# The first stage of a two-layer trunk in a written order on four engines

## The chip, the cores and the metric

The kernel runs on one core of one Trainium2 chip. The metric is the device time of one execution in microseconds (us); lower is better. Before the change the median of three runs is 1106.1 us (1105.2 to 1107.23). TensorE (PE) multiplies matrices, ScalarE (ACT) applies functions and copies, VectorE (DVE) does elementwise work, GpSimd (POOL) sets memory, SyncE's queue (SP) issues the loads.

## What is computed

Two layers over 512 tokens of width 1024. Each layer is a token mixer and a SwiGLU feed-forward, each between two norms and with a shift, a scale and a gate from a condition `c`. Only the opening of layer 0 is touched:

```
shift, scale, gate = split(silu(c) @ w + b)      # w: 1024 x 3072
h = rms_norm(x, g) * (1 + scale) + shift         # x: 512 x 1024
qkv = h @ w_qkv                                  # then stick-breaking attention
```

## The kernel before, in words

Every product is made in three passes: an operand is split into a high half (ScalarE copies it to fp32r) and a low half (VectorE subtracts the high one from the original), and `mm3` multiplies high by high, high by low and low by high.

The first stage makes, from x and c, the transposed and modulated h (eight blocks of 128 columns, each 128x512, as high and low half), and multiplies it at once: half of v (four banks, 512 columns each, for the four token tiles) and q and k of the first pair of heads (one bank each). So each of the eight blocks k has twelve passes for v (`v_step`, L706) and six for q and k (`qk0_step`, L795), all 128x128 by 128x512.

- `norm0` (L678) squares a token tile of x on ScalarE, takes the root (`rms`, L467), and scales the tile on VectorE. `turn0` (L687) turns all eight of its 128x128 blocks on TensorE into two banks and copies them to the tiles `xhT` on ScalarE (VectorE for half of the first two token tiles).
- The scale and shift of a block are sums over the 1024 rows of an ada weight, weighted by silu(c). For blocks 0 and 1, `row0` (L764) does the sum on TensorE: sixteen instructions (eight calls) with a one-column operand, a copy of the row to SBUF, and two small products that turn it; `scales` (L777) adds and multiplies. For blocks 2 to 7, in pairs, `ada0_sum` (L740) sums on VectorE, eight steps of 512 columns into one accumulator, and `cols0` (L748) and `sums0` (L754) turn it with small products on TensorE; a VectorE product gives `ab`.
- `h0` (L784) writes h (high half) and x once more with scale and shift, both on ScalarE, and the low half on VectorE.
- Loads are issued by `load` (L125) from SyncE's queue. Weights pass through `wload` and `wemit` (L144, L154): a raw tile of 512 KB (two buffers), high half, low half.
- `bg0` is a background job (`Bg`, L397) that sums the gate of layer 0 in eight VectorE steps of 1024 columns, a few steps at a time; its loads come three steps ahead.

The framework orders instructions of one engine by program order and readiness. A helper keeps an order by hand where its `chain` flag is set: `dve`, `act` and `pe_op` (L64 to L101) tie each instruction to the one before on that engine. Before the change no chain is on in the first stage.

Around the stage, `for b in range(1, 4)` at L820 runs over the pairs of blocks; the loop over k = 6, 7 behind it finishes the products. Then v, q and k are copied out, and the second v half starts.

Of the kernel before, what the change touches and what calls it, by code (L numbers as in the profile page):

```python
# [13 lines left out]
P = 128  # L14
# [19 lines left out]
def trunk(ctx: ExitStack, tc: tile.TileContext, A: dict, out: bass.AP):  # L34
# [85 lines left out]
    def mm3(o, lh, ll, rh, rl, start, stop):  # L120
        mm(o, lh, rh, start, False)
        mm(o, lh, rl, False, False)
        mm(o, ll, rh, False, stop)

    def load(dst, src):  # L125
        nc.sync.dma_start(out=dst, in_=src)

    def split(hi, lo, src, hi_dve=False):
        if hi_dve:
# [24 lines left out]
    def wemit():  # L154
        n = len(got)
        src, a, b, key = stream[n]
        if len(raws) == n:
            wload()
        if src is None:
            if not first_blocks or n > first_blocks[-1] + KF:  # L160
                first_blocks.append(n)
            for _ in blocks(*next_raws(n)):
                pass
            return
        raw = raws[n]
        if key[0] == "wdn" and key[2] in SEVEN[key[1]]:
            got.append(down_blocks(raw))
            return
        h, l = wtile(a, b, SHORT if key[0] in ("wgu", "win_u") else 16)
        if key[0] == "wqk" and key[1]:  # L170

            act.activation(h[:], raw[:], AF.Copy)
            nc.vector.tensor_tensor(l[:], raw[:], h[:].bitcast(F32), ALU.subtract)
            if len(raws) == n + 1 and stream[n + 1][3][0] == "wqk":
                wload()
        else:
            high = act.activation(h[:], raw[:], AF.Copy)
            last_low[0] = nc.vector.tensor_tensor(l[:], raw[:], h[:].bitcast(F32), ALU.subtract)  # L178
# [178 lines left out]

    cT = consts.tile([P, KD], F32, name="cT")
    load(cT[:], A["c"])
    x0, a0 = [], []  # L360
    for tt in range(NT):
        xt = slot(F32, "x0", 1, 1024)
        load(xt[:, 0, :], A["x"][tt * P : (tt + 1) * P, :])
        x0.append(xt[:, 0, :])
        if tt == 0:
            identt = consts.tile([P, P], F32, name="identt")
            load(identt[:], A["consts"][:, 0, :])
            cols = consts.tile([P, 4, KD], F32, name="cols")
            load(cols[:], A["cols"])
        elif tt == 3:  # L370
            a0.extend(ada0_raw(0, q) for q in range(2))
    wload()
# [294 lines left out]


    add = consts.tile([P, KD, 2], F32, name="add")
    dve.tensor_copy(add[:, :, 1], cols[:, 1, :])  # L670
    dve.tensor_scalar(add[:, :, 0], cols[:, 0, :], 1.0, None, ALU.add)
    mul = consts.tile([P, KD, 2], F32, name="mul")
    dve.memset(mul[:, :, 1], 1.0)
    dve.tensor_copy(mul[:, :, 0], cols[:, 2, :])

    xhT = [slot(F32, "xhT") for _ in range(4)]

    def norm0(tt):  # L678
        xt = x0[tt]
        junk = npool.tile([P, D], F32, tag="n", name=nm("junk"))  # L680
        sx = small.tile([P, 1], F32, tag="sx", name=nm("sx"))
        act.activation(junk[:], xt, AF.Square, accum_out=sx[:])
        sd, r1 = rms(sx[:])
        dve.reciprocal(r1[:], sd[:])
        dve.tensor_scalar(xt, xt, r1[:, 0:1], None, ALU.mult)

    def turn0(tt):  # L687
        xt = x0[tt]
        for q in range(2):
            ps = bank("tp0")  # L690
            for k in range(4):
                kk = q * 4 + k
                transpose(ps[:, k * P : (k + 1) * P], xt[:, kk * P : (kk + 1) * P])
            for k2 in range(2):
                dst = xhT[q * 2 + k2][:, :, tt * P : (tt + 1) * P]
                src = ps[:, k2 * 256 : (k2 + 1) * 256].rearrange("p (a b) -> p a b", a=2)
                if q and tt < 2:
                    dve.tensor_copy(dst, src)
                else:
                    act.activation(dst, src, AF.Copy)  # L700

    hT = new_hT()

# [33 lines left out]

    onec = oneb[:, 0:1]

    def ada0_sum(raws, n, nk, tag="acch"):  # L740
        acc = adas.tile([P, 512], F32, tag=tag, name=nm("acc"))
        nc.gpsimd.memset(acc[:, :n], 0.0)
        for q, raw in enumerate(raws):
            for k in range(nk):
                ada_stt(acc[:, :n], raw[:, k, :], q * nk + k)
        return acc

    def cols0(k):  # L748

        ps = bank("ab0", "p")  # L750
        mm(ps[:, 0:4], ident, add[:, k : k + 2, :].rearrange("p n a -> p (n a)"), True, False)
        return ps

    def sums0(ps, acc, k):  # L754

        for i in range(4):
            mm(ps[:, i : i + 1], acc[:, i * P : (i + 1) * P], onec, False, i == 3)
        ab = small.tile([P, 2, 2], F32, tag="ab", name=nm("ab"))
        dve.tensor_tensor(
            ab[:], ps[:, :4].rearrange("p (n a) -> p n a", a=2), mul[:, k : k + 2, :], ALU.mult  # L760
        )
        return ab

    def row0(raws):  # L764

        ps = bank("ab0", "p")
        for q, raw in enumerate(raws):
            for k in range(4):
                mm(ps[0:1, :256], sc[:, q * 4 + k : q * 4 + k + 1], raw[:, k, :], q + k == 0, q * 4 + k == 7)
        row = stp.tile([P, 256], F32, tag="row", bufs=2, name=nm("row"))  # L770
        dve.tensor_copy(row[0:1, :], ps[0:1, :256])
        ps = bank("ab0", "p")
        for i in range(2):
            mm(ps[:, i : i + 1], row[0:1, i * P : (i + 1) * P], oneb[0:1, 0:1], True, True)
        return ps

    def scales(ps, k):  # L777

        ab = small.tile([P, 2, 2], F32, tag="ab", name=nm("ab"))
        dve.tensor_tensor(ab[:, 0, :], ps[:, :2], add[:, k, :], ALU.add)  # L780
        dve.tensor_tensor(ab[:, 0, :], ab[:, 0, :], mul[:, k, :], ALU.mult)
        return ab

    def h0(ab, i, k):  # L784

        xk = xhT[k // 2][:, k % 2, :]
        h, l = hTk(hT, k, 0, T)
        for out in (h, xk):
            act.activation(out, xk, AF.Identity, scale=ab[:, i, 0:1], bias=ab[:, i, 1:2])
        dve.tensor_tensor(l, xk, h.bitcast(F32), ALU.subtract)  # L790

    wv0, wqk0 = [], []

    def qk0_step(k):
        for w, pb in zip(wqk0, (pq0, pk0)):  # L795
            h, l = hTk(hT, k, 0, T)
            mm3(pb[:], w[0][:, k, :], w[1][:, k, :], h, l, k == 0, k == KD - 1)

    norm0(0)
    norm0(1)  # L800
    turn0(0)
    norm0(2)
    ab0 = row0(a0)
    turn0(1)
    norm0(3)
    turn0(2)
    turn0(3)
    wv0.append(wget(("wv", 0, 0), 0))
    a2 = [ada0_raw(2, q) for q in range(4)]
    h0(scales(ab0, 0), 0, 0)  # L810
    ab1 = row0(a1)
    wqk0.append(wget(("wqk", 0, 0), 0))
    vb = [bank("v0") for _ in range(NT)]
    pq0, pk0 = bank("pq"), bank("pk")
    v_step(vb, 0, 0, wv0[0])
    h0(scales(ab1, 1), 0, 1)
    wqk0.append(wget(("wqk", 0, 1), 0))
    wload()
    acc = ada0_sum(a2, 512, 2)
    for b in range(1, 4):  # L820

        ps = cols0(2 * b)
        if b > 1:
            v_step(vb, 0, 2 * b - 2, wv0[b - 1])
        qk0_step(2 * b - 2)
        an = [ada0_raw(b + 2, q) for q in range(4)] if b < 3 else []
        if b == 1:
            v_step(vb, 0, 1, wv0[0])
        ab = sums0(ps, acc, 2 * b)
        h0(ab, 0, 2 * b)  # L830
        wv0.append(wget(("wv", 0, b), 0))
        h0(ab, 1, 2 * b + 1)
        if b < 3:
            wload()
            acc = ada0_sum(an, 512, 2, ("acch", "accl")[b % 2])
        if b > 1:
            v_step(vb, 0, 2 * b - 1, wv0[b - 1])
        if b == 2:
            bg0.step(3)
        qk0_step(2 * b - 1)  # L840
        if b == 3:
            bg0.step(1)
    for k in (6, 7):
        v_step(vb, 0, k, wv0[3])
        bg0.step(1)
        qk0_step(k)
        bg0.step(1)
# [9 lines left out]
    with tc.tile_pool(name="att", bufs=1) as att, tc.tile_pool(name="att2", bufs=2) as att2:  # L857
# [196 lines left out]
        for k in range(KD):  # L1054
            if k % 2 == 0:
                wv = wget(("wv", 1, k // 2))
            v_step(vb, 1, k, wv)
            if k in (3, 5):
                cur[0](B31 if k == 3 else B2)
            if k in (1, 2, 6):  # L1060
                bg0.step(1)
# [615 lines left out]
```

## Time and profile before

| | |
|---|---|
| span of the profiled execution | 1104.6 us |
| runs | 1106.1 us median, 1105.2 to 1107.23 |
| busy: TensorE, VectorE, ScalarE, GpSimd | 98%, 86%, 54%, 3% |
| first transpose on TensorE | 7.84 us |
| first v product | 23.72 us |
| first product of the second v half | 62.41 us |
| bytes moved | 176.38 MB, 160 GB/s mean |

Rows of a timeline read: start, duration (of the whole group where a count xN stands), engine, line, operation, output tile <- input tiles, shapes, count, and in brackets how long the engine was idle before and what released it. A line is often that of a helper (L109 is every matmul), so go by the tiles: `ab` holds scales, `acc` the sums of ada rows, `wh` and `wl` the high and low halves of a weight, `hTh` and `hTl` of h, `tp` turned blocks, `vf` and `q` the copies out. Matmuls are pipelined, so the distance between starts is their price, not the duration. Rows of the stretches read: busy time and instructions of PE, PEld (weight loads), DVE, ACT and POOL, then granted TensorE clock, busy share of the DMA engines and GB/s.

### The profile page before, as it was taken

The numbers are of one execution on the slowest core, as the hardware profiler recorded it, in microseconds if no ns is written. First come the engines' busy times: TensorE is split into PE (matmuls) and PEld (weight loads), VectorE is DVE, ScalarE is ACT, GpSimd is POOL, SyncE is SP. The second block draws the span as 40 slices with busy tenths as digits, with TensorE's granted clock in tenths as the row PEclk, the third lists the DMA queues.
The fourth block names the chain that finished last, engine by engine and source line by source line (L and its number), as shares of the span: only waits on it lengthen the run. The fifth ranks groups of instructions, "written<-read, shape, count | busy, mean of one in ns | idle before, by whom it ended". The sixth has DMA issues, their size and how long they took to land.

```text
span 1104.6 us, 18512 instructions
## 1 busy us (share of the span) xinstructions
PE 1085.9 (98%) x7404; PEld 979.0 (89%) x7404; DVE 945.9 (86%) x1248; ACT 594.2 (54%) x982; POOL 29.5 (3%) x53
## 2 busy tenths in 40 slices
PE   6999999999999999999999999999999999999997
PEld 4787788788999999998888889988999999989996
DVE  4988999966989999989866967668979999899997
ACT  6554665665655555554243626426555555565662
POOL 0020100000000000000000000001000000000000
PEclk9999999999999999999999999999999999999999
DMA  8976434304433434359757465334334343333252
GB/s 302 370 226 217 142 116 133 125 11 152 157 112 131 162 119 146 132 197 351 272 191 256 144 205 196 96 116 155 128 117 155 128 159 102 110 115 96 77 187 81
DMA packets 51355, 176.38 MB, mean 160 GB/s; under 512 B 6074, under 2 KB 9146, under 8 KB 51268
## 3 DMA queue, kind: packets, MB, share of 16 engines
q1 hardware_dynamic: 48708, 166.81, 44.6%
q0 software_dynamic: 2560, 8.39, 2.1%
q8 instruction: 58, 0.95, 0.3%
q14 instruction: 29, 0.24, 0.1%
HBM read 164.69 MB, written 8.39 MB: 157 GB/s over the span
## 4 chain that ended last, share of the span: by engine, by line
PE 90%; DVE 4%; DMA 2%; ACT 2%; issue 1%; SPq 0%; DVEq 0%; ACTq 0%
PE r L109 32%; PE y L109 18%; PE pqk L109 7%; PE gu L109 6%; PE v L109 5%; PE X L109 4%; PE u L109 4%; PE Y L109 3%; PE av L109 2%; PE z L109 2%; PE tw L117 1%; PE tp L117 1%; PE Z L109 1%; PE W L109 1%; PE ab L109 1%
## 5 line engine op out<-in xcount | busy, mean ns | idle before, releaser
L87 ACT ACTIVATE wh<-raw 128x1024 fp32r<-128x1024 f32 (+1 forms) x112 | 115.7, 1038 | 130.5 <-PE y L109 39.4
L109 PE MATMUL r<-Sh,wh 128*128 128x256 f32 x608 | 168.1, 276 | 0.5 <-ACT e L87 0.5
L109 PE MATMUL r<-Sh,wl 128*128 128x256 f32 x608 | 167.9, 276 | 0.0
L109 PE MATMUL r<-Sl,wh 128*128 128x256 f32 x608 | 167.9, 276 | 0.0
L109 PE MATMUL y<-wh,as 128*128 128x512 f32 x480 | 149.9, 390 | 0.0
L178 DVE TENSOR_TENSOR wl<-raw,wh 128x1024 fp32r<-128x1024 f32 x87 | 105.8, 1222 | 48.2 <-ACT wh L87 47.6
L109 PEld LDWEIGHTS r<-Sh,wh 128*128 128x128 f32 x608 | 114.1, 188 | 1.0 <-ACT e L87 0.9
L109 PEld LDWEIGHTS r<-Sl,wh 128*128 128x128 f32 x608 | 114.1, 188 | 0.1
L109 PEld LDWEIGHTS r<-Sh,wl 128*128 128x128 f32 x608 | 114.1, 188 | 0.0
L109 PEld LDWEIGHTS y<-wh,as 128*128 128x128 f32 x480 | 90.0, 188 | 18.6
L71 DVE TENSOR_TENSOR wl<-f,wh 128x1024 fp32r<-128x1024 f32 x87 | 103.2, 1220 | 0.0
L87 ACT ACTIVATE wh<-f 128x1024 fp32r<-128x1024 f32 x87 | 91.8, 1055 | 15.3 <-DVE f L71 11.6
L87 ACT ACTIVATE e<-r 128x256 f32<-128x256 f32 x114 | 43.7, 385 | 101.8 <-PE r L109 100.8
L109 PE MATMUL y<-wl,as 128*128 128x512 f32 x240 | 93.7, 391 | 0.0
L109 PE MATMUL r<-hTh,wh 128*128 128x256 f32 x304 | 84.2, 277 | 0.2 <-DVE gu L71 0.2
L109 PE MATMUL r<-hTl,wh 128*128 128x256 f32 x304 | 84.0, 276 | 0.0
L109 PE MATMUL r<-hTh,wl 128*128 128x256 f32 x304 | 84.0, 276 | 0.0
L109 PE MATMUL r<-hTh,b 128*128 128x256 f32 x304 | 57.9, 276 | 0.0
L109 PEld LDWEIGHTS r<-hTh,wh 128*128 128x128 f32 x304 | 57.1, 188 | 0.9 <-DVE gu L71 0.9
L109 PEld LDWEIGHTS r<-hTh,wl 128*128 128x128 f32 x304 | 57.1, 188 | 0.0
L109 PEld LDWEIGHTS r<-hTl,wh 128*128 128x128 f32 x304 | 57.1, 188 | 0.0
L87 ACT ACTIVATE wh<-rawx 128x1024 fp32r<-128x1024 f32 x38 | 40.4, 1063 | 29.8 <-PE r L109 29.0
(262 smaller groups left out, 2937.1 us busy)
## 6 DMA issues: line engine op xcount, KB each, us to landing
rawada<-in_ada SPq DMA_DIRECT2D x80, 512.0 KB, 5.7
rawy<-in_wy SPq DMA_DIRECT2D x38, 512.0 KB, 4.6
rawx<-in_wx SPq DMA_DIRECT2D x38, 512.0 KB, 3.7
raw<-in_wdown SPq DMA_DIRECT2D x22, 512.0 KB, 5.4
raw<-in_wdn SPq DMA_DIRECT2D x22, 512.0 KB, 3.6
raw<-in_wqk SPq DMA_DIRECT2D x16, 512.0 KB, 3.9
ada<-in_ada0p SPq DMA_DIRECT2D x12, 512.0 KB, 6.3
raw<-in_wgu SPq DMA_DIRECT2D x12, 512.0 KB, 3.5
```

The source lines that it names most:

```text
L71: b = getattr(nc.vector, op)(*args, **kw)
L87: b = nc.scalar.activation(*args, **kw)
L109: b = nc.tensor.matmul(o, l, r, start=start, stop=stop, skip_group_check=True)
L117: last_tp[0] = nc.tensor.transpose(o, i, ident)
L178: last_low[0] = nc.vector.tensor_tensor(l[:], raw[:], h[:].bitcast(F32), ALU.subtract)
```

## The change

The whole first stage is written out in one order, and the chains of TensorE, ScalarE, VectorE and now also of the load queue are on throughout it.

- Loads: the first ada block comes right behind the first x tile, the second ahead of the last x tile; the first v weight is loaded in two halves; the q and k weights have tiles of their own (`rawq`); the four blocks of the first pair sum stand between them.
- Scales of blocks 0 and 1: three of the four ada blocks are summed on VectorE (four steps of 256 columns each); the remaining one (`a1[0]`) still goes over TensorE as a row.
- `spin(12)`: twelve matmuls of zeros ahead of everything on TensorE.
- `turn0` turns only blocks 0 and 1, into two banks `xp` that are kept until h is written from them. `turn1` turns the other six; for token tiles 2 and 3 only after the v products of blocks 0 and 1.
- The products go pass by pass over the four token tiles (`v_pass`, `qk_pass`) instead of three passes per token tile. The third q and k passes of blocks 0 and 1 are put off.
- The sums of a pair's scales are turned in one call (`cols0`); for the last pair it lies between the v and the q, k products of block 5.
- The gate steps of `bg0`: three at pair 2 (loads alone), two behind block 7's low half, two at the end, and one more in the second v half; 3 + 1 + 4 before.

```diff
 def load(dst, src):
-    nc.sync.dma_start(out=dst, in_=src)
+    b = nc.sync.dma_start(out=dst, in_=src)
+    if sp["chain"]:
+        if sp["prev"] is not None:
+            order(b, sp["prev"])
+        sp["prev"] = b
...
+    def high0(ab, i, k):
         xk = xhT[k // 2][:, k % 2, :]
+        src = xp[k][:] if k < 2 else xk
+        for out in (hTk(hT, k, 0, T)[0], xk):
+            last = act.activation(
+                out, src, AF.Identity, scale=ab[:, i, 0:1], bias=ab[:, i, 1:2]
+            )
+        if k == 1:
+            last_sqrt[0] = last
...
+    def both(k, late=None):
+        for t in range(3):
+            v_pass(t, k)
+        if late is not None:
+            late()
+        for t in range(3):
+            qk_pass(t, k)
...
+    pe["chain"] = act.chain = dve.chain = True
+    spin(12)
+    acc = acc0(256, "acch")
+    square0(0)
+    sum0(acc, a0[0], 4, 0)
...
+    scale0(0)
     turn0(0)
+    copies = [turn1(0, "b")]
+    square0(1)
+    scale0(1)
     turn0(1)
+    copies.append(turn1(1, "b"))
+    square0(2)
+    sum0(acc, a0[1], 4, 4)
+    scale0(2)
     turn0(2)
+    square0(3)
+    ab0 = cols0(acc, 0, 1)
+    scale0(3)
     turn0(3)
+    ps = bank("ab0", "p")
+    for k in range(4):
+        mm(ps[0:1, :256], sc[:, k : k + 1], a1[0][:, k, :], k == 0, k == 3)
+    high(wv0[0][0][:, 0, :], rawv[:, 0, :])
+    copies[0]()
+    low(wv0[0][1][:, 0, :], rawv[:, 0, :], wv0[0][0][:, 0, :])
+    copies[1]()
+    high0(ab0, 0, 0)
+    high(wv0[0][0][:, 1, :], rawv[:, 1, :])
     vb = [bank("v0") for _ in range(NT)]
+    v_pass(0, 0)
+    v_pass(1, 0)
+    acc = acc0(256, "accl")
+    sum0(acc, a1[1], 4, 4)
+    low0(0)
+    row = stp.tile([P, 256], F32, name="row")
+    dve.tensor_copy(row[0:1, :], ps[0:1, :256])
+    low(wv0[0][1][:, 1, :], rawv[:, 1, :], wv0[0][0][:, 1, :])
+    ab1 = cols0(acc, 1, 1, row)
+    v_pass(2, 0)
+    high(wqk0[0][0], rawq[0][:])
+    high0(ab1, 0, 1)
+    high(wqk0[1][0], rawq[1][:])
+    acc = acc0(512, "acch")
+    sum0(acc, pair[0], 2, 0)
+    low0(1)
+    for q in range(1, 4):
+        sum0(acc, pair[q], 2, 2 * q)
+    for t in range(3):
+        v_pass(t, 1)
     pq0, pk0 = bank("pq"), bank("pk")
+    for tt in (2, 3):
+        copies.append(turn1(tt, "p"))
+        copies[tt]()
+    for k in range(2):
+        for t in range(2):
+            qk_pass(t, k)
     for b in range(1, 4):
+        nxt = None
+        ab = cols0(acc, 2 * b) if b == 1 else ab2
+        wv0.append(wget(("wv", 0, b), 0))
+        if b < 3:
+            nxt = [ada0_raw(b + 2, q) for q in range(4)]
+            wload()
         if b == 1:
+            for w, raw in zip(wqk0, rawq):
+                low(w[1], raw[:], w[0])
+            for k in range(2):
+                qk_pass(2, k)
+        high0(ab, 0, 2 * b)
+        low0(2 * b)
+        high0(ab, 1, 2 * b + 1)
+        both(2 * b)
...
+            sum0(acc, nxt[0], 2, 0)
+        low0(2 * b + 1)
...
```

More of the change, by code (lines that the diff above doesn't have):

```diff
@@ L359, in trunk @@
     load(cT[:], A["c"])
+    identt = consts.tile([P, P], F32, name="identt")
+    cols = consts.tile([P, 4, KD], F32, name="cols")
     x0, a0 = [], []
+    sp["chain"] = True
     for tt in range(NT):
@@ L687, in turn0 @@
+    xp = [bank("xp") for _ in range(2)]
     def turn0(tt):
[L688 to L700, printed above, removed]
+        for k in range(2):
+            transpose(xp[k][:, tt * P : (tt + 1) * P], x0[tt][:, k * P : (k + 1) * P])
@@ L702, in trunk, with spin @@
+    zero = stp.tile([P, 256], F32, name="zero")
+    dve.memset(zero[:], 0.0)
+    def spin(n):
+        ps = bank("spin")
+        for _ in range(n):
+            mm(ps[:, 0:256], zero[:, 0:P], zero[:], True, True)
     hT = new_hT()
@@ new lines, in low0, with high, low, v_pass @@
+    def low0(k):
+        h, l = hTk(hT, k, 0, T)
+        dve.tensor_tensor(l, xhT[k // 2][:, k % 2, :], h.bitcast(F32), ALU.subtract)
+    def high(t, raw):
+        act.activation(t, raw, AF.Copy)
+    def low(l, raw, h):
+        dve.tensor_tensor(l, raw, h.bitcast(F32), ALU.subtract)
+    def v_pass(t, k):
+        h, l = hTk(hT, k, 0, T)
+        w = wv0[k // 2]
+        a, b = ((h, w[0]), (h, w[1]), (l, w[0]))[t]
+        for tt in range(NT):
+            mm(
+                vb[tt][:], a[:, tt * P : (tt + 1) * P], b[:, k % 2, :],
+                k + t == 0, k == KD - 1 and t == 2,
+            )
@@ L838, in trunk @@
         if b == 2:
             bg0.step(3)
[L840 to L847, printed above, removed]
+        if b < 3:
+            ab2 = late[0] if late else cols0(acc, 2 * b + 2)
+    bg0.step(2)
+    pe["chain"] = act.chain = dve.chain = sp["chain"] = False
     cc = stp.tile([P, P], F32, name="cc")
@@ L1060, in trunk @@
             if k in (1, 2, 6):
-                bg0.step(1)
+                bg0.step(1 + (k == 2))
             elif k in (0, 4, 7):
```

148 lines of the change are left out of this document (68 added, 80 removed).

## The prediction

> **What bounds the kernel now.** I read the page's busy shares first, then stretches of the span by engine, then the first 65 us engine by engine.
>
> ```profile
> PE 1085.9 (98%) x7404; PEld 979.0 (89%) x7404; DVE 945.9 (86%) x1248; ACT 594.2 (54%) x982; POOL 29.5 (3%) x53
> ...
> 0.00:23.70 23.70, 15.02 (x68) 8.18 (x68) 7.85 (x25) 16.40 (x32) 1.19 (x6) 1.00 0.87 335
> 23.70:62.40 38.70, 38.11 (x179) 30.75 (x179) 37.27 (x50) 18.38 (x25) 5.75 (x12) 1.00 0.81 298
> 62.40:95.00 32.60, 32.60 (x154) 25.50 (x152) 27.60 (x29) 17.01 (x28) 4.83 (x9) 1.00 0.81 262
> ```
>
> TensorE is busy 98% of 1104.6 us, and from 62.4 to 95 us all 32.6 us of 32.6. So where the first stage hands over to the second v half (62.41 below), nearly every microsecond won or lost travels on to the end. Before 23.7 us it did 15.0 us of work, none of it the q, k and v products; from 23.7 to 62.4 VectorE too is busy, 37.27 of 38.7 us.
>
> ```profile
> 7.84 1.97 PE L117 MATMUL tp<-identt,x 128*128 128x128 f32 x8 [7.84 <-DVE x L71]
> ...
> 12.55 5.12 PE L109 MATMUL ab<-ada,sc 128*1 128x256 f32 x16
> ...
> 18.82 1.42 PE L117 MATMUL tp<-identt,x 128*128 128x128 f32 x11
> 20.17 3.61 PE L109 MATMUL ab<-ada,sc 128*1 128x256 f32 x16
> 23.72 0.50 PE L109 MATMUL v<-wh,hTh 128*128 128x512 f32 x1
> ...
> 42.41 0.95 PE L109 MATMUL ab<-oneb,acc 128*128 128x1 f32 x8
> 43.22 0.48 PE L109 MATMUL pk<-hTh,wh 128*128 128x512 f32 x1
> ...
> 44.46 0.50 PE L109 MATMUL v<-wh,hTh 128*128 128x512 f32 x1 [0.31 <-ACT hTh L87]
> ...
> 58.33 0.39 PE L109 MATMUL v<-wh,hTh 128*128 128x512 f32 x1
> ...
> 62.41 0.39 PE L109 MATMUL v<-wh,hTh 128*128 128x512 f32 x1
> ```
>
> These are TensorE's rows. The products begin at 23.72, right behind two groups of sixteen that multiply ada rows by the condition (5.12 and 3.61 us). From 58.33 to 62.41 lie 18 products of one 128x512 pass: 0.227 us each. The stage has 8 x (12 v + 6 qk) = 144, which is 32.6 us; 23.72 to 62.41 is 38.7, so 6.1 us there are small sums and waits. The change can attack 23.72 and those 6.1 us.
>
> VectorE and ScalarE give the prices:
>
> ```profile
> 9.64 0.17 DVE L71 RECIPROCAL r<-sd 128x1 f32<-128x1 f32 x1 [1.86 <-ACT sd L87]
> 9.84 0.75 DVE L71 TENSOR_SCALAR x<-x,r 128x1024 f32<-128x1024 f32 x1
> ...
> 17.70 0.41 DVE L71 COPY row<-ab 1x256 f32<-1x256 f32 x1 [3.43 <-PE ab L109]
> ...
> 37.44 4.68 DVE L71 SCALAR_TENSOR_TENSOR acc<-ada,sc,acc 128x512 f32<-128x512 f32 x6
> ...
> 43.39 0.16 DVE L71 TENSOR_TENSOR ab<-ab,mul 128x4 f32<-128x4 f32 x1
> ...
> 46.51 1.29 DVE L71 TENSOR_TENSOR hTl<-xhT,hTh 128x512 fp32r<-128x512 f32 x2
> ...
> 58.18 6.57 DVE L71 SCALAR_TENSOR_TENSOR G<-rawada,sc,G 128x1024 f32<-128x1024 f32 x5
> ...
> 66.39 2.36 DVE L178 TENSOR_TENSOR wl<-raw,wh 128x1024 fp32r<-128x1024 f32 x2 [0.45 <-ACT wh L87]
> ```
>
> ```profile
> 8.13 1.06 ACT L87 ACTIVATE junk<-x 128x1024 f32<-128x1024 f32 x1 [1.78 <-DMA x<-in_x]
> ...
> 9.31 0.29 ACT L87 ACTIVATE sd<-sx,epsb 128x1 f32<-128x1 f32 x1
> ...
> 19.41 1.76 ACT L87 ACTIVATE xhT<-tp 128x256 f32<-128x256 f32 x6 [0.46 <-PE tp L117]
> ...
> 22.61 1.04 ACT L87 ACTIVATE wh<-raw 128x1024 fp32r<-128x1024 f32 x1
> ...
> 43.59 1.52 ACT L87 ACTIVATE hTh<-xhT,ab 128x512 fp32r<-128x512 f32 x2 [5.44 <-DVE ab L71]
> 45.02 1.51 ACT L87 ACTIVATE xhT<-xhT,ab 128x512 f32<-128x512 f32 x2
> ```
>
> One sum step of 512 columns comes every 0.79 us ((4.68-0.75)/5, with 0.75 for a single one), one of 1024 every 1.3 us. A low half of 1024 columns comes every 1.14 us, of 512 every 0.6. Reciprocal and row scale: 0.95. Square to root: 1.47 (8.13 to 9.60). ScalarE: 1.05 for a high half of 1024, about 0.3 per turned copy, and for the pair that writes h and x again 0.71 between starts, 0.81 to the end.
>
> ```profile
> 2.60 5.51 DMA x<-in_x
> ...
> SPq L126 <- DMA x<-in_x: 2.9, 3, 1.0
> SPq L126 <- DMA ada<-in_ada0s: 1.8, 2, 0.9
> ...
> 9.37 0.33 SPq L126 DMA_DIRECT2D ada<-in_ada0p  x1
> ...
> 10.64 0.33 SPq L126 DMA_DIRECT2D ada<-in_ada0p  x1
> ...
> 11.87 0.33 SPq L126 DMA_DIRECT2D ada<-in_ada0p  x1
> ...
> 13.11 0.33 SPq L126 DMA_DIRECT2D ada<-in_ada0p  x1
> ```
>
> Loads: x block 1 lands at 8.11. The load queue then waits for the landing of two more x blocks and of two ada0s blocks before each further issue, so these landed at about 9.4, 10.6, 11.9 and 13.1: one 512 KB block per 1.25 us, in the order of issue.
>
> **The change, part by part.** Everything is now in a fixed order on TensorE, ScalarE, VectorE and the load queue, so I follow the four queues through it. Times are positions in the span of the profiled execution.
>
> *Loads.* The first ada block moves ahead of the identity, cols and x 1; the second ahead of x 3. By slots: ada 0 about 8.0, x 1 9.4, x 2 10.6, ada 1 11.9, x 3 13.1. Then half a v block 13.7, row blocks 15.0 and 16.2, the other half 16.8, wq 18.1, four pair blocks to 23.1, and wk only at 24.3.
>
> *Front.* The two row products on TensorE (5.12 + 3.61 us) shrink to four matmuls; the rest becomes twelve 256-column sum steps on VectorE. No row shows that size; half a 512 step is 0.39 and all of it 0.79, and the step from 1024 to 512 (1.3 to 0.79) continued gives 0.53, which I take: 2.1 us per four. They stand in VectorE's queue ahead of the scale of x, which waits behind them: ada 0 at 8.0, sums to 10.1, three small copies to 10.4, scale 0 to 11.3, scale 1 to 12.3, sums of ada 1 to 14.3, scale 2 to 15.3. Then TensorE turns two blocks (0.5) and forms the first shift and scale (0.7), VectorE multiplies (0.16), and only behind that scale 3 runs: 16.6 to 17.6. Two turns, and ScalarE writes the first h from PSUM at 18.1 to 18.9. Products start at 18.9 instead of 23.72: 4.8 us won. The twelve spinning matmuls lie in TensorE's idle time before the first turn (7.84 us idle now) and cost nothing, nor does the set-to-zero behind them; without that cover they would cost at most a 5.12 us group scaled by 12/16, 3.8 us.
>
> *Second block.* VectorE from 17.6: low half 0.6, four row sums 2.1, low of h 0.6, row copy 0.41, low half 0.6, to 21.9; the small sums and their product to 22.5; h of block 1 at 23.3. The 24 v products of both blocks are done at 26.0.
>
> *Turns that were put off.* Twelve turns of x 2 and x 3 now follow on TensorE. They have two banks: six turns (0.7), two copies before the first bank is free (0.7), six more (0.8): 28.2. ScalarE cannot copy sooner by much: ahead of the copies in its queue stands the high half of wk, landed 24.3, done 25.4. Eight qk products: 30.0. Small sums at 30.2.
>
> *The new wait.* VectorE multiplies these at 31.2 to 31.3 (43.39 against 42.41 gives 0.98 + 0.16). Behind it in VectorE's queue stand three low halves, wv 1, wq, wk: 2 x 1.14 + 1.22 = 3.5 us, to 34.8. The last four qk products of blocks 0 and 1 need the last two. TensorE is through with the small sums at 31.0 (0.8 after 30.2) and, but for one product, waits until 34.8, with all of blocks 2 to 7 queued behind. It then has 3 + 108 products: 35.5 after the three.
>
> *The tail.* Blocks 2 and 3: 36 x 0.227 = 8.2, to 43.7. Small sums, product, h of block 4: in the rows, sums at 42.41 let v begin at 44.46, so 2.05 + 0.13 for the identity term: 45.9. Block 4 and the v of block 5: 6.8, to 52.7. VectorE meanwhile has, from 45.0: a low half, a wait for x, low of h, eight sums, low of h: 1.1 + 1.1 + 0.6 + 6.3, to 54.1. Sums 0.8, qk of block 5 1.4, blocks 6 and 7 8.2: 64.5. The copies it no longer does (four, from PSUM) fell in its idle front.
>
> So the stage ends at 64.5 against 62.41, 2.1 us later: 4.8 won at the start, and 6.9 lost. The products themselves and the bytes are unchanged.
>
> *Gate sums behind.* Now eight 1024 steps run on VectorE within or just behind the stage; afterwards four have run by 64.5 and four (5.3 us) lie among the second v half. There VectorE is busy 27.6 of 32.6 us, so 5.0 are free; 0 to 1.3 us could show, and I take 0.3. One more or fewer step per k of gate loads moves nothing else on the load queue: 512 KB takes 1.25 us, and from 62.4 to 95 the DMA share is 0.81.
>
> Sum: 2.1 + 0.3 = 2.4 us. The profiled span of 1104.6 lies 1.5 below the median of the three runs, 1106.1; adding the difference to the median gives 1108.5.
>
> What can be off: the 256-column step (0.39 to 0.79: -1.7 to +3.1 us on the twelve, of which only the first eight reach the start of products, and of that start only what exceeds the wk landing counts); the landings (half a slot, 0.6). On the low side wk's landing is a floor: its high half at 25.4, two copies and six turns to 27.0, eight products, sums at 29.0, and from sums to stage end is 34.3 us by the steps above: 63.3, 0.9 us late. On the high side sums at 32 give 66.3, 3.9 us late.
>
> **A clock that is not in the clock column.** The granted clock reads 1.00 in all three stretches, yet sixteen equal matmuls took 5.12 us at 12.55 and 3.61 at 20.17, and eight turns 1.97 us at 7.84 against eleven in 1.42 at 18.82. Being cold cost the first group 1.5 us. The Trainium skill, page "TensorE: Matmul & The Clock Gate", Part 1, says that the array runs at half rate until some 3.4 us of sustained work and returns to half rate after an idle window of that length. The trace agrees with the first half; no row here shows the second. By that rule the wait of 3.8 us in the new order, broken by one product, is a danger the sum above leaves out; it is a rival.
>
> **Forecast and rivals.** The forecast is the sum as it stands, with the small sums of the second pass beginning between 29 and 32: 1107 to 1110, and 2.2 us late (0.2%, about what a measurement of this kernel can tell from no change) lies inside that. Chance 0.55, of it 0.32 above the 2.2 us and 0.23 below.
>
> 1. *The lead survives* (other side: faster). It decides at the small sums of the second pass: at 28.1 instead of 30.2 the stage ends at 62.4 (1106.1), at 26.0 at 60.3 (1104.0). For it: TensorE loses 8.7 us of row products, and VectorE works only 7.85 of the first 23.7 us. Against it: wk by its slot lands at 24.3, so the place would have to be some 3 us ahead of what the load order gives, and the three low halves keep their 3.5 us wherever they begin. Faster by over 0.2%: 0.15.
> 2. *Won and lost cancel*: TensorE waits for wk's landing alone, the floor of 63.3 or up to 0.9 us less, and the gate steps hide: 1106.1 to 1107.0. For it: ScalarE has nothing else to do between the h of block 1 and wk. Against it: turns and copies share two banks. Chance 0.15.
> 3. *TensorE turns cold in the new wait.* The stretch behind it then runs at half rate until it is warm, 1.5 us by the two sixteens: stage end 66.0, total 1110.0; with a second such stretch at the start of the products, 1111.5. For it: one matmul alone breaks the wait. Against it: the waits of 1.24 us and less in the trace show no such fall. Chance 0.10.
> 4. *The gate steps stand ahead of a weight.* The low half of the second v half's first weight is issued outside the order and may fall behind the last two gate steps, 2.6 us, of which TensorE would wait about 1.3: 1109.8. Chance 0.05.
>
> **How the numbers follow.** Slower by over 0.2%: 0.32 + 0.10 + 0.05 = 0.47; within: 0.23 + 0.15 = 0.38; faster: 0.15. The forecast is the likeliest case, so 1108.5. For eight in ten the range reaches down into the first rival, to the sums at 27 (61.3, 1.1 us early, less 0.5 for the landings: 1104.5), and up past the cold case to 1112.
>
> **What the changed profile would show.** Right: first v product near 19 us; wk's high half at 24.3; in TensorE's rows a hole of 3 to 4 us ahead of the last four qk products of blocks 0 and 1, released by VectorE's low half; two further waits, about 1.2 us for h of block 4 and 1.4 for the sums of blocks 6 and 7; second v half from 63.3 to 66. Wrong in the front: products before 17.5 or after 20.5. Wrong in the middle: no hole, or the hole released by ScalarE or a load. Wrong behind: the second v half begins late as computed, yet the end does not follow, so later waits took it up. Cold: passes after the hole 0.43 apart.

## The result: 8.8 us slower

The changed kernel takes 1114.76 us at the median (1113.74 to 1116.24) against 1105.99 (1105.2 to 1107.23) in the same comparison: ratio 1.0085, 95% interval 1.0071 to 1.0099. I had forecast 1108.5 and a range up to 1112.0, so the sign was right and the size outside the range. The profiled span went from 1104.6 to 1113.5 us, 8.9 more. The busy shares of the changed kernel:

```profile
PE 1092.9 (98%) x7412; PEld 986.1 (89%) x7412; DVE 949.8 (85%) x1255; ACT 594.1 (53%) x983; POOL 30.2 (3%) x55
```

TensorE is busy 7.0 us longer than before (1092.9 against 1085.9). The matmuls of zeros, in time that was idle, are 6.98 of it; the row products fell from 8.73 to 3.56; so other work takes 5.2 us more. 3.4 of them are the same products taking longer in two stretches (worked out below); the rest lies in small sums and turns. The next view, stretches of the changed kernel (columns as before: length, PE, PEld, DVE, ACT, POOL, granted clock, DMA share, GB/s), shows why that is possible.

```profile
10.00:15.00 5.00, 3.11 (x18) 2.47 (x15) 3.68 (x8) 3.96 (x12) 0.00 (x0) 0.63 1.03 413
...
18.00:21.60 3.60, 3.60 (x10) 0.86 (x9) 2.46 (x6) 2.89 (x4) 0.00 (x0) 0.51 1.03 420
21.60:33.90 12.30, 11.69 (x65) 9.61 (x64) 7.71 (x12) 6.50 (x11) 0.53 (x1) 1.00 1.03 419
...
38.10:42.20 4.10, 4.10 (x11) 3.18 (x10) 3.99 (x6) 0.53 (x2) 0.00 (x0) 0.53 0.07 25
42.20:51.90 9.70, 8.60 (x43) 7.20 (x42) 3.89 (x7) 1.83 (x3) 0.00 (x0) 1.00 0.00 0
51.90:55.80 3.90, 3.90 (x11) 3.02 (x10) 3.83 (x6) 3.30 (x4) 0.00 (x0) 0.56 0.93 285
```

In three stretches (from 18.0, 38.1 and 51.9 us) TensorE is busy all the time and yet runs at a granted clock of 0.51, 0.53 and 0.56. In the rows of the kernel before the clock read 1.00 throughout the stage. TensorE's own rows:

```profile
1.30 6.98 PE L109 MATMUL spin<-zero 128*128 128x256 f32 x24 [1.30 <-DVE zero L71]
...
18.09 3.56 PE L109 MATMUL ab<-ada,sc 128*1 128x256 f32 x8
21.58 1.20 PE L109 MATMUL v<-wh,hTh 128*128 128x512 f32 x4
...
32.83 1.03 PE L109 MATMUL ab<-oneb,acc 128*128 128x1 f32 x8
36.40 0.80 PE L109 MATMUL pq<-hTh,wl 128*128 128x512 f32 x1 [2.53 <-DVE wl L71]
37.53 0.79 PE L109 MATMUL pk<-hTh,wl 128*128 128x512 f32 x1 [0.34 <-DVE wl L71]
38.12 0.63 PE L109 MATMUL pq<-hTh,wl 128*128 128x512 f32 x1
...
42.22 1.09 PE L109 MATMUL v<-wh,hTl 128*128 128x512 f32 x4
...
48.77 1.03 PE L109 MATMUL ab<-oneb,acc 128*128 128x1 f32 x8
50.91 1.20 PE L109 MATMUL v<-wh,hTh 128*128 128x512 f32 x4 [1.10 <-ACT hTh L87]
51.94 1.65 PE L109 MATMUL v<-wl,hTh 128*128 128x512 f32 x4
...
55.82 0.39 PE L109 MATMUL pq<-hTl,wh 128*128 128x512 f32 x1
...
70.31 0.39 PE L109 MATMUL v<-wh,hTh 128*128 128x512 f32 x1
```

Read the distances between starts. From 38.12 to 42.22 ten 128x512 products take 4.10 us; at the 0.227 of the kernel before they would take 2.27. From 51.94 to 55.82 ten more take 3.88. Both stretches follow a wait: 2.53 us with 0.34 behind one product, and 1.10 us behind one-column sums. The second v half starts at 70.31 instead of 62.41, 7.9 us late. The last 1.0 us of the span is lost behind it. These are all the waits of TensorE from 61 to 335 us in the kernel before, and then in the changed kernel (total, times, longest):

```profile
PE av L109 <- DVE ar L71: 0.8, 1, 0.8
PE r L109 <- ACT e L87: 0.5, 1, 0.5
PE av L109 <- ACT ar L87: 0.4, 1, 0.4
```

```profile
PE av L109 <- DVE accl L71: 1.0, 1, 1.0
PE av L109 <- DVE ar L71: 0.8, 1, 0.8
PE av L109 <- ACT ar L87: 0.4, 1, 0.4
PE r L109 <- ACT e L87: 0.3, 1, 0.3
PE v L109 <- DVE wl L185: 0.2, 1, 0.2
```

A matmul of the gate sums (`accl`) now waits 1.0 us for VectorE, a wait that the kernel before has not.

### The profile page after: what moved, and what is told of

Same layout as the page of the kernel before. It is cut to its first block, busy times and chain, and to the rows that moved or that the text cites. A ratio compares the mean times of both kernels' runs of the same rounds, so it can differ in the third digit from the quotient of the medians.

```text
span 1113.5 us, 18540 instructions
## 1 busy us (share of the span) xinstructions
PE 1092.9 (98%) x7412; PEld 986.1 (89%) x7412; DVE 949.8 (85%) x1255; ACT 594.1 (53%) x983; POOL 30.2 (3%) x55
## 4 chain that ended last, share of the span: by engine, by line
PE 87%; DVE 5%; DMA 3%; ACT 2%; issue 1%; POOL 0%; SPq 0%; DVEq 0%; ACTq 0%
PE r L109 30%; PE y L109 18%; PE pqk L109 7%; PE v L109 6%; PE X L109 4%; PE u L109 4%; PE gu L109 3%; PE Y L109 3%; PE av L109 2%; PE z L109 2%; PE tw L117 1%; PE Z L109 1%; PE W L109 1%; PE tp L117 1%; DMA raw<-in_wqk 1%
## 5 line engine op out<-in xcount | busy, mean ns | idle before, releaser
L87 ACT ACTIVATE wh<-raw 128x1024 fp32r<-128x1024 f32 (+2 forms) x111 | 113.9, 1030 | 136.2 <-PE y L109 38.7
L185 DVE TENSOR_TENSOR wl<-raw,wh 128x1024 fp32r<-128x1024 f32 x81 | 98.5, 1222 | 46.7 <-ACT wh L87 46.0
```

Source lines behind the costliest of these rows:

```text
L87: b = nc.scalar.activation(*args, **kw)
L185: last_low[0] = low_engine.tensor_tensor(l[:], raw[:], h[:].bitcast(F32), ALU.subtract)
```

## The experiments

The theory under test: TensorE's clock falls to half after the new waits, and that doubles what the waits cost. The rival: the waits and the length of VectorE's queue alone cost the time, and the clock is a companion. "Stage end" is the first product of the second v half: 62.41 us before, 70.31 after. The first gate-and-up product of the feed-forward part is at 277.3 and 286.6.

### Zero matmuls in the two holes

```diff
                 low(w[1], raw[:], w[0])
+            spin(5, "p")
             for k in range(2):
                 qk_pass(2, k)
...
             ab2 = late[0] if late else cols0(acc, 2 * b + 2)
+            if b == 1:
+                spin(2, "p")
```

> The changed kernel with matmuls of zeros put into two holes of TensorE's order: five behind the small sums of the second pass (ahead of the put-off third q and k passes) and two behind the small sums of block 4; nothing else is moved. Theory clock: TensorE falls to half rate behind these holes (2.53 us at 33.9, and 1.1 us with the small sums before it at 48.8) and the products after each cost 1.8 and 1.6 us more; filled, the clock column stays at 1.00 from 21.6 us on, and the second v half starts at about 66.9 instead of 70.3, the kernel is 3.4 us faster than the changed one (1111.3). Theory order: the products behind the holes wait for VectorE and ScalarE anyway and the half rate is hidden; the second v half starts at 70 or later, since the zeros only add work (1114 to 1115).

Measured: 1113.19 us, ratio to the kernel before 1.0067 (1.0052 to 1.0082); stage end 68.76, first gate-and-up product 283.5. Stretches of this kernel:

```profile
33.90:42.00 8.10, 7.20 (x31) 5.44 (x30) 7.96 (x11) 4.13 (x6) 0.91 (x2) 1.00 0.38 132
...
50.00:56.00 6.00, 5.53 (x26) 4.51 (x24) 5.79 (x9) 2.67 (x3) 0.00 (x0) 1.00 0.92 339
56.00:62.00 6.00, 5.47 (x21) 4.51 (x22) 4.45 (x7) 3.15 (x4) 3.42 (x8) 0.72 0.61 192
```

and TensorE's row at the start of the last one:

```profile
56.53 1.05 PE L109 MATMUL ab<-oneb,acc 128*128 128x1 f32 x8 [0.99 <-DVE acc L71]
```

The clock is 1.00 behind both filled holes, so here work without any use keeps it up. But with blocks 2 to 5 faster, the sums of blocks 6 and 7 come later on VectorE than TensorE needs them: a wait of 0.99 us, and the clock falls there (0.72). Of the 3.4 us that the two half-rate stretches cost, 1.6 came back, and 0.5 of that was there ahead of the first fill (small sums at 32.30 instead of 32.83). Both theories have a part: the clock follows the waits, and VectorE's queue makes the next wait.

### The two low halves ahead of the scale product

The product that gives the scales of blocks 2 and 3 waits for TensorE's small sums; wq's and wk's low halves stood behind it in VectorE's queue. Here they stand ahead.

```diff
         nxt = None
+        if b == 1:
+            for w, raw in zip(wqk0, rawq):
+                low(w[1], raw[:], w[0])
         ab = cols0(acc, 2 * b) if b == 1 else ab2
...
-            for w, raw in zip(wqk0, rawq):
-                low(w[1], raw[:], w[0])
             for k in range(2):
                 qk_pass(2, k)
```

> The changed kernel with the low halves of wq and wk moved in VectorE's order ahead of the scale product of blocks 2 and 3, into the 2.0 us where VectorE waits for the small sums; the put-off q and k passes stay where they are. Theory order: the hole of TensorE from 33.9 to 36.4 and 37.5 goes but for 0.4 us, 3.3 us won. Theory clock: with the hole goes the half rate behind it too, 1.8 us more, so 5.1 in all: second v half at 65.2, kernel at 1109.7; by the order alone 67.0 and 1111.5. The half rate at block 4 stays in either.

Measured: 1109.3 us (1106.98 to 1112.06), ratio 1.0031 (1.002 to 1.0043); stage end 65.92, first gate-and-up product 280.4. Of the single edits this gains most over the changed kernel, 5.5 us. TensorE's waits from 30 us to the end of the stage:

```profile
45.51 1.20 PE L109 MATMUL v<-wh,hTh 128*128 128x512 f32 x4 [1.10 <-ACT hTh L87]
...
53.74 1.05 PE L109 MATMUL ab<-oneb,acc 128*128 128x1 f32 x8 [1.01 <-DVE acc L71]
```

The hole is gone. The wait of 1.10 at 45.51 is there and the granted clock stays at 1.00 from 42 to 50 us; only the one of 1.01 at 53.74 is followed by a fall (0.77 from 56 to 62). So a short wait sometimes brings the clock down and sometimes not. Against the changed kernel the fall behind the hole is gone, and the one at block 4 has moved to blocks 6 and 7.

### Zero matmuls in the front

```diff
     copies = [turn1(0, "b")]
+    spin(2, "p")
...
     copies.append(turn1(1, "b"))
+    spin(2, "p")
...
     ab0 = cols0(acc, 0, 1)
+    spin(3, "p")
     scale0(3)
```

> The changed kernel with matmuls of zeros in TensorE's waits of the front: two behind each of the first two groups of turns, three behind the first small sums. Theory clock: the eight row matmuls at 18.1 run at full rate, 1.8 us instead of 3.5, the first v product is at 19.9 instead of 21.6 and the second v half at 68.6 (1113.0). Theory order: the first products come earlier but wait for the row copy, the scale product of block 1 or the load of wk, and the second v half is at 70.3 within 0.5.

Measured: 1113.92 us, ratio 1.0073 (1.0057 to 1.009); stage end 67.21. TensorE's rows of the row products and of the first v products, and two stretches:

```profile
17.10 1.89 PE L109 MATMUL ab<-ada,sc 128*1 128x256 f32 x8
18.92 1.20 PE L109 MATMUL v<-wh,hTh 128*128 128x512 f32 x4
```

```profile
15.00:21.60 6.60, 6.60 (x35) 4.55 (x35) 5.03 (x11) 4.38 (x10) 0.53 (x1) 1.00 1.03 420
21.60:30.00 8.40, 7.83 (x41) 6.23 (x41) 6.70 (x10) 6.55 (x11) 0.53 (x1) 1.00 1.03 418
```

The eight row instructions take 1.89 us instead of 3.56, which is the half rate, and they begin 1.0 us earlier, because the turns and small sums ahead of them are shorter too. The first v product is at 18.92 instead of 21.58, and the small sums of the second pass begin at 30.18 instead of 32.83. The stage ends 3.1 us earlier, though the clock falls behind the hole and behind block 4's wait as before. Of these 3.1 only 0.8 reach the span (1112.7): in the first block that is made with seven products (`r`), TensorE waits 2.2 us for ScalarE at 320 us, and the ten us behind have a clock of 0.83. That wait is taken up below.

### No zero matmuls at the start

```diff
-    spin(12)
```

> The changed kernel without the twelve matmuls of zeros at the start. Theory clock: they end at 8.3 and the clock falls at about 11.8 all the same, ahead of the row matmuls and the products, so they buy nothing: second v half at 70.3 within 0.5 and 1114.8 within 1. If they do keep the front warm, turns get slower (six in 1.5 instead of 0.8) and the stage ends 0.5 to 1.5 later. If TensorE instead counts work since a cold start, the turns from 9.5 on warm it by 15 and the rows run fast: up to 1.7 us earlier.

Measured: 1115.94 us, ratio 1.0095 (1.0078 to 1.0113); stage end 70.41, 0.1 behind the changed kernel, and the eight row instructions take 3.57 us, as slow as with the spinning (3.56). So the spinning buys nothing at the stage end: the clock has come down again in the front's gaps (0.63 from 10 to 15 us in the changed kernel) before the first long products. The median is 1.2 us longer than that of the changed kernel, but the two intervals overlap, so that it costs or saves anything in all is not shown.

### The kernel before with zero matmuls at its start

```diff
+    spin(12)
     norm0(0)
     norm0(1)
...
     turn0(0)
+    spin(2)
     norm0(2)
```

> The kernel before with matmuls of zeros added on TensorE, twelve at the start and two behind the first turned token tile; nothing else. Theory clock: the old kernel too paid for a cold array, in its first turns and in the first sixteen row matmuls (5.12 us against 3.61 for the second sixteen). Warm, the second v half starts at 61 instead of 62.4 and the kernel takes 1104.7 instead of 1106.2. If the front of the old kernel is bound by the loads of x and by VectorE, nothing moves: 62.4 and 1106.2 within 0.5.

Measured: 1106.0 us, ratio 1.0 (0.9988 to 1.0012). TensorE's rows:

```profile
12.25 3.61 PE L109 MATMUL ab<-ada,sc 128*1 128x256 f32 x16
...
18.38 3.61 PE L109 MATMUL ab<-ada,sc 128*1 128x256 f32 x16
21.92 0.50 PE L109 MATMUL v<-wh,hTh 128*128 128x512 f32 x1
```

The first sixteen row matmuls take 3.61 us instead of 5.12: the kernel before ran a part of them, about seven by the 0.21 us that each of the changed kernel's eight loses (3.56 against 1.89), at half rate while its clock column read 1.00. The stage ends at 60.56, 1.85 earlier, the first gate-and-up product comes 1.0 earlier, the span is 0.6 shorter, and the median is the same. A lead of 1.85 us at the end of the stage was not a lead at the end. Behind the stage three of TensorE's waits have grown: the gate matmul waits 1.0 us for VectorE (nothing before), a turn 0.4 (nothing before), and the block with seven products 0.9 instead of 0.5.

### The written order switched off

```diff
-    pe["chain"] = act.chain = dve.chain = True
     spin(12)
...
-    sp["chain"] = True
     for tt in range(NT):
```

> The changed kernel with the four hand-written chains off in the first stage: the same instructions in the same program order, but each engine's instructions placed by readiness. Theory order: the queue behind the scale product is what costs, and placed by readiness the low halves of wq and wk come before it: the hole of 2.5 us at 33.9 goes, with the half rate behind it; second v half at 65 to 67, kernel at 1109 to 1112. If the work itself is too much for VectorE, the stage ends at 70 as it does now, 1114 to 1115.

Measured: 1117.4 us (1113.55 to 1120.84), ratio 1.0092 (1.0063 to 1.0122); stage end 71.48. Two stretches:

```profile
15.00:26.00 11.00, 10.75 (x35) 6.92 (x36) 6.92 (x15) 7.22 (x15) 1.05 (x2) 0.50 1.03 421
26.00:34.00 8.00, 5.32 (x15) 3.61 (x14) 7.86 (x11) 2.89 (x5) 0.00 (x0) 0.71 1.03 419
```

The framework's own order is no better: half rate from 15 to 26 us and a wait of 2.68 us at 30. The forecast of 65 to 67 missed, and 71.48 is nearer to its rival, too much work for VectorE. But the same work fits into a stage that ends at 61.01 in the reordered kernel below. So a fixed order as such is not shown to cost anything; the place of two low halves does (above).

### The two good edits together, and a reordered tail

The first of these two has the low halves first, the warm front and two zero matmuls behind the sums of block 4. The second has the first two, and moves the sums of block 4 between block 3's v and q, k products and the first quarter of the sums of blocks 6 and 7 ahead:

```diff
-        both(2 * b + 1, (lambda: late.append(cols0(acc, 2 * b + 2))) if b == 2 else None)
+        both(2 * b + 1, (lambda: late.append(cols0(acc, 2 * b + 2))) if b < 3 else None)
...
+            if b == 1:
+                acc3 = acc0(512, "acch")
+                sum0(acc3, n3[0], 2, 0)
```

> The changed kernel with the low halves of wq and wk ahead of the scale product, zeros in the waits of the front, and two matmuls of zeros behind the small sums of block 4. Theory clock and order together: from the 65.9 of the version with low halves first, 1.7 us less for the warm row matmuls; the fill at block 4 only moves the wait to the sums of blocks 6 and 7, where VectorE is about 1 us late. Second v half at 64.2, kernel at 1107.5. By the order alone the warm front changes nothing: 65.9 and 1109.3.

> The changed kernel with the low halves first, the warm front, the small sums of block 4 moved between the v and the q, k products of block 3 (as they are for blocks 6 and 7), and the first quarter of the sums of blocks 6 and 7 made ahead of that, where VectorE waits; its two loads come earlier by the same. Both theories: the wait of 1.1 us for h of block 4 goes, and the wait of 1.0 us for the sums of blocks 6 and 7; from 64.2 the second v half comes to 62.0, kernel at 1105.3, no slower than the one before. If half rate still strikes somewhere: 63.5 and 1107.

Measured, the first: 1108.53 us, ratio 1.002 (1.0006 to 1.0035), stage end 63.56; as expected, the wait moved to the sums of blocks 6 and 7 (0.99 us), and the clock fell there (0.72 from 52 to 58 us). The second: 1108.99 us, ratio 1.0023 (1.0012 to 1.0034), stage end 61.01, which is 1.4 earlier than in the kernel before and 9.3 earlier than in the changed one. Its clock reads 1.00 through the whole stage. And yet it is slower than the kernel before. The two longest of its waits from 61 to 335 us:

```profile
PE r L109 <- ACT e L87: 2.2, 1, 2.2
PE av L109 <- DVE accl L71: 1.9, 1, 1.9
```

The gate matmul now waits 1.9 us for VectorE, and the block with seven products waits 2.2 us for ScalarE at 320 us. In the changed kernel, whose stage ends 9.3 us later, these are 1.0 and 0.3; in the kernel before 0 and 0.5.

The second wait has its root some 20 us earlier, in VectorE's wait for a load:

```profile
298.84 1.23 DVE L71 TENSOR_TENSOR f<-rawx,rawy 128x1024 f32<-128x1024 f32 x1 [2.22 <-DMA rawx<-in_wx]
...
319.91 0.39 PE L109 MATMUL r<-Sh,wh 128*128 128x256 f32 x1 [2.16 <-ACT e L87]
```

Between the two VectorE pauses only once, for 0.26 us, and ScalarE, which TensorE waits for, itself waits for VectorE. In every trace where this wait is not filled the two differ by 0.2 us at most: 0.63 and 0.49 us in the kernel before, 0.29 and 0.3 in the changed one, 0.42 and 0.34 with the low halves first, 1.78 and 1.7 with the two holes filled, 2.39 and 2.20 with the warm front.

### Those two waits taken away

The second pair of gate matmuls comes later in TensorE's order (the trace has 21 products between the pairs instead of 12, so three groups of three, 2.0 us, and not the four of the expectation); in the second kernel eighteen unread matmuls of 128x256 stand in the wait at 320 us as well; the third is the kernel before with zero matmuls at its start and the later gate pair.

```diff
-            fill(n, (2, 6))
+            fill(n, (2,) if n == 8 else (1, 3, 6))
```

```diff
             act.activation(s5, R3, AF.Copy)
-            product(R1, "2", "T2", False, False)
+            if f == NH and self.li == 0:
...
+                for i in range(18):
+                    mm(ps[:, :256], wh, h, True, True)
...
+            else:
+                product(R1, "2", "T2", False, False)
```

> The version with the low halves first, the warm front and the earlier sums, which ended its first stage at 61.01 us and still took 1109.0, and one change: the second pair of gate matmuls in the attention part comes four groups of three matmuls (2.7 us) later in TensorE's order. Theory A (the stage's gain is lost in a few waits behind it, the first of them this pair's wait of 1.9 us for VectorE): the wait is gone, the first gate-and-up product is at 276.4 instead of 278.2, the time 1107.2. Rival B (VectorE is behind by a fixed amount, so that the next wait takes its place): a wait of 1 to 2 us appears at another line before 278, the first such product stays within 0.5 of 278.2, and the time is 1108.5 to 1109.5.

> The same, and eighteen matmuls of 128x256 whose result nothing reads (about 2.0 us at full rate) where TensorE waited 2.2 us for ScalarE at 320 us, ahead of the fifth product of the first block with seven products. Theory A: the granted clock is 1.00 in 320 to 330 us instead of 0.83, which gives 1.7 us back beside the 1.8 of the later gate pair: 1105.5. Rival C (the wait is longer than the fill, or the clock falls in spite of it): the clock stays at 0.8 to 0.9 there and the time is 1107 or more. Where the wait has become shorter than the fill by itself, the fill costs up to 1.5 us.

> The kernel before with zero matmuls while x arrives (which ended its first stage at 60.56 us and took 1106.0), and the same later place of the gate pair, which waited 1.0 us there. Theory A: the first gate-and-up product is at 275.3 instead of 276.3 and the time 1105.0. Rival B: another wait of 0.5 to 1.0 us takes its place, and the time stays at 1106.0.

Measured: 1108.57 us, ratio 1.0026 (1.0013 to 1.0039); 1108.41 us, ratio 1.003 (1.0014 to 1.0045); 1105.91 us, ratio 1.0006 (0.9996 to 1.0015). In the first the gate wait is gone and no other takes its place before 277: from stage end to the first gate-and-up product it is 215.1 us (61.66 to 276.78) instead of 217.2. But the profiled execution is one of the shorter of its twelve runs (1107.13 us), and the median stays where the rival had it. In the second the wait at 320 is filled and the clock there is 1.00, as expected, but its stage ended 0.9 later, and its time, too, is the rival's (1107 or more). In the third the rival was right: another wait of 1.4 us for VectorE, ahead of the q, k products, took the place of the one removed, and the first gate-and-up product stayed at 276.32. At 318 us this third kernel waits 2.0 us for ScalarE, again behind a wait of VectorE for the load (2.13). No version beats the kernel before.

The first two have the same first stage, instruction for instruction, and show the clock at work. TensorE's rows of the first, then of the second, and a stretch of each:

```profile
40.87 1.05 PE L109 MATMUL ab<-oneb,acc 128*128 128x1 f32 x8 [0.98 <-DVE acc L71]
...
46.09 0.39 PE L109 MATMUL pq<-hTh,wh 128*128 128x512 f32 x1
```

```profile
40.85 1.05 PE L109 MATMUL ab<-oneb,acc 128*128 128x1 f32 x8 [0.98 <-DVE acc L71]
...
47.58 0.40 PE L109 MATMUL pq<-hTh,wh 128*128 128x512 f32 x1
```

```profile
42.00:46.00 4.00, 4.00 (x18) 3.12 (x18) 2.53 (x5) 3.56 (x5) 0.00 (x0) 1.00 0.38 106
```

```profile
42.00:46.00 4.00, 4.00 (x12) 3.01 (x12) 2.54 (x5) 3.58 (x5) 0.00 (x0) 0.62 0.39 99
```

The same wait of 0.98 us ahead of the same eight one-column sums, within 0.02 us of the same place. In one execution the clock stays at 1.00 and the products reach the next q at 46.09; in the other it falls (0.62) and they reach it at 47.58, 1.5 us later. So a wait of this size does not decide whether the clock falls. The Trainium skill, page "TensorE: Matmul & The Clock Gate", Part 1, calls the window in which the hardware counts activity free-running, so that the number of slow matmuls differs from one execution to the next. These two traces fit that, in the middle of a kernel; no run here shows the window itself.

## Why the prediction was wrong

*Right.* VectorE's front: four sum steps of 256 columns take 2.05 us (I took 2.1), the last scale of x stands at 16.39 to 17.4 (16.6 to 17.6). Two landings were not as forecast, without effect: the first ada block's sums start at 6.38 (8.0), and wk's high half runs at 26.44, behind h of block 1 in ScalarE's queue and not at the landing (24.3). From the first v product to the second pass's small sums I had 11.3 us, measured 11.25 (21.58 to 32.83). The hole stands where I put it and for the reason that I gave, as VectorE's rows of the changed kernel show:

```profile
6.38 2.05 DVE L71 SCALAR_TENSOR_TENSOR acc<-ada,sc,acc 128x256 f32<-128x256 f32 x4 [5.13 <-DMA ada<-in_ada0s]
...
16.39 0.15 DVE L71 RECIPROCAL r<-sd 128x1 f32<-128x1 f32 x1
16.58 0.83 DVE L71 TENSOR_SCALAR x<-x,r 128x1024 f32<-128x1024 f32 x1
...
33.90 0.16 DVE L71 TENSOR_TENSOR ab<-ab,mul 128x4 f32<-128x4 f32 x1 [2.03 <-PE ab L109]
33.98 1.23 DVE L71 TENSOR_TENSOR wl<-raw,wh 128x1024 fp32r<-128x1024 f32 x1
35.12 2.35 DVE L71 TENSOR_TENSOR wl<-rawq,wh 128x1024 fp32r<-128x1024 f32 x2
```

The scale product of 33.90 has three low halves behind it, 3.5 us in all, and the last put-off k product begins 4.70 us after the small sums (4.6 in the sum). The wait ahead of block 4's v is 1.10 (about 1.2). The other wait that I had forecast, 1.4 us for the sums of blocks 6 and 7, is not there (59.61 without a wait): TensorE was slow enough for VectorE to catch up. In the four versions above in which the clock did not fall behind block 4's wait (holes filled, low halves first, no zeros at the start, the first of the two combined), it appears, with 0.99 to 1.01 us.

*Wrong: "products start at 18.9".* Two errors in one term. "Shrink to four matmuls" counted calls; each call is two instructions, so eight stand in the row, 1.8 us at full rate by the second group of sixteen in the profile before. (The same slip stands in the bound of 3.8 us for the spinning: it is 24 instructions and 6.98 us, which the idle time did cover.) And they ran at half rate, 3.56 us from 18.09. ScalarE was done with h of block 0 at 18.76 as forecast:

```profile
17.98 0.78 ACT L87 ACTIVATE hTh<-xp,ab 128x512 fp32r<-128x512 f32 x1 [1.54 <-PE xp L117]
```

so v waited for the row products, not for h: 21.58 instead of 18.9, 2.7 us of the miss. With the warm front it is at 18.92, so the half rate is the whole of it: 1.7 us in the row products (1.89 against 3.56) and 1.0 ahead of them. That 18.92 meets the forecast is luck in part, since the row products still take 1.0 us more than the four that I counted.

*Wrong: "the tail", 34.8 to 64.5.* I priced its 108 products at 0.227 each. From the hole's end to the stage end I had 29.7 us; it took 32.8 (37.53 to 70.31). The two stretches at half rate are 1.8 and 1.6 us beyond full rate, and the product at 37.53 ahead of the first takes 0.59 to the next start, 0.4 too much. Against these 3.8 stand the 1.4 us of the wait that did not come; some 0.7 of small differences make up the 3.1. With the front's 2.7 and 0.1 in the middle that is 5.9, which is 70.31 against 64.5 but for rounding. So the step that failed is the price of full rate for every product: the fall of the clock, which the sum put at nothing.

*Wrong: how the cold case was weighed.* I had the mechanism as the third rival, at 1.5 us for each stretch, close to the 1.6 to 1.8 measured, but gave it 0.10 and at most two stretches. There were three: the row products, behind the hole, behind block 4's sums. The reason I gave against it, that waits of 1.24 us and less in the trace before show no fall, does not hold: the wait of 1.24 us is that of the weight loads at 10.65, ahead of eight turns that took 1.97 us like the first eight, so TensorE was still slow there and nothing could fall. Behind that place the longest wait of TensorE in that trace is 0.8 us. And it was one execution; the pair of traces above shows how little one says. In the changed kernel a wait of 1.10 us behind about 1 us of one-column sums was enough, and one of 2.53 with a product and 0.34 behind it. The Trainium skill, same page, section "Why this matters for your kernels", asks for no idle gaps over about 3 us; here shorter ones brought the clock down, and the measurement decides.

*Wrong: "gate sums behind", 0.3 us.* VectorE is late with the gate, and its price was 1.0: a wait at `accl`, where I had looked for it at the low half of the first weight (0.2 there). That the moved gate steps make this wait is not shown: the version with the low halves first has the same steps and no such wait.

*Settled and open.* The clock is shown as a cause: filling a hole or the front with useless matmuls brings it back to 1.00 and the stage ends earlier, by 1.6 and 3.1 us. So is the order of the low halves, by 5.5 us of the total. With these and the reordered tail together, the stage end is earlier than in the kernel before, so the delay within the stage is accounted for. Of the 8.8 us of the total only some 6 came back, though. What stays open is why leads gained in the stage are lost behind it. The gate pair's wait is one place; taking it away did not shorten the median. The wait at 320 us is another; the clock fell behind it in four traces (0.83 to 0.87) and stayed at 1.00 in two others, with waits of 1.7 and 2.06 us. That wait follows the landing of a load, as shown, and not the size of the lead: it is 0.3 us with a stage end of 65.92 and 1.7 with 68.76. Why that load lands late was not tried: issuing it earlier would tell.

## What to carry to other kernels

In an engine that is busy 98% a new wait of one or two microseconds can cost more than its length, because the clock can fall behind it: here a fall cost 1.5 to 1.8 us each time. Carry it as a term of its own for each new wait, and do not take a stage without falls as proof that there will be none. Where a product waits for a short reply from another engine, look at what stands behind that reply in the queue: two low halves moved ahead of one small product were worth 5.5 us here. Do not count a lead at the end of a stage as a lead at the end of the kernel: 1.4 and 1.85 us were gone here, in waits for VectorE and ScalarE that had not been there or had been shorter.

## What the hardware showed that I had not expected

- Matmuls of zeros kept the granted clock at 1.00 like any others where they stood in the gap itself; twelve at the start alone were worth 0.1 us at the stage end.
- Ahead of the first rise the clock column reads 1.00 for work that runs at half rate: sixteen row matmuls took 5.12 us under 1.00 in the kernel before, and 3.61 with zero matmuls ahead of them; without the spinning the changed kernel's eight took 3.57 under 1.00.
- Turns and one-column sums with gaps between them do not hold the clock: it was 0.63 from 10 to 15 us of the changed kernel, with TensorE busy 3.11 of 5.
- The same wait of 0.98 us in the same instructions cost 1.5 us more in one execution than in another. The times of the kernel with the later gate pair range from 1105.7 to 1113.91.
